# Grouped-query attention: probabilities times values in plain float32 on two column tiles, once per query tile

## The chip, the cores and the metric

The kernel runs on one core of a Trainium2 chip. The metric is the device time of one execution in microseconds (us), smaller is better. The time before is the median of three runs, 1531.39 us (1531.35 to 1532.13).

## The reference

One encoder block works on `x` of 1024 positions and 1024 channels, in float32. `x` is normalised and projected by one wide matrix; three attention branches follow (a dilated window, grouped-query attention, cross-attention to a memory of 256 rows), each is multiplied with a gate and projected, the three are merged by sigmoid gates, and a last projection closes the block. The change touches the grouped-query attention alone: eight query heads of 64 channels share two key and value heads, without a mask, over all 1024 keys.

```python
qb_ = axial_rope(rms_norm(bq.reshape(b, s, B_HEADS, HEAD_DIM), q_norm[layer]), row_pos, col_pos)
kb_ = axial_rope(rms_norm(bk.reshape(b, s, B_KV_HEADS, HEAD_DIM), k_norm[layer]), row_pos, col_pos)
vb_ = bv.reshape(b, s, B_KV_HEADS, HEAD_DIM)

def attend(qc, kb_=kb_, vb_=vb_):
    sc = jnp.einsum('bqkgd,bskd->bkgqs', qc, kb_).astype(jnp.float32) * (HEAD_DIM ** -0.5)
    p = jax.nn.softmax(sc, axis=-1).astype(vb_.dtype)
    return jnp.einsum('bkgqs,bskd->bqkgd', p, vb_)
```

## The kernel before

**Precision by splitting.** Most products run in a reduced float32 (`R`, float32r) of which two parts are kept: `split` (L104 to L106) writes a rounded part with ScalarE (ACT, L105) and the rest with VectorE (DVE, L106). A product of two split operands is three matmuls, high by high, high by low, low by high (`dense`, L143, L145, L147; `passes`, L125). The projection of the input, `dense`, has 24 matmuls of 512 columns for one half of a unit of 128 output channels, and 48 for the unit.

**The stages.** First the keys and values of the grouped-query attention (`kv_proj`, L370, with their finishing in `k_norm` and `kn_mult`), the memory's keys and values and the memory attention. Then the grouped-query attention (`b_att`, from L678 on, about 228 to 572 us of the profile). Then the dilated attention (`a_att`, `pv` at L987), the merging of the branches, and the output projection.

**Order.** TensorE's order (PE) is the program's own: a generator issues instructions and yields a cost in ns. `weave` runs two generators side by side, a queue of projection units (`dense`) and an attention; it always continues the one that is behind in its share of the whole cost. So an attention step that yields a large cost is followed by as much projection. The other engines' order is set by the tile framework's scheduler; the attention's instructions have a higher priority. Only the first part, up to the end of `kv_gen`, has ACT, DVE and POOL in program order as well.

**The values.** `kn_mult` writes the values of key tile T as `VS[:, T]`, for each of the two value heads 128 columns: the rounded part of the 64 channels (ACT, L407) and its rest (DVE, L408).

**The attention.** Keys stand on the partitions. One visit `i` is a query tile T of 128 positions and one key head, thus four query heads: 512 columns. A visit goes over eight key tiles of 128 keys in eight ticks `n`, and 128 ticks make the stage. Of different visits, one tick does these things:

- `row_max` (L688, L689): one matmul of scores with the queries on the partitions, and a minimum over 512 keys on DVE. After eight, L691 joins them.
- `shift`, nine ticks after a visit's first maximum: a transpose of the extremes (L696) and a DVE instruction (L697) that puts them beside the queries' low parts, `QL`.
- `scores`, ten ticks after: two matmuls (L706, and L707, which reads `QL`) into one PSUM bank, and the exponential on ACT (L709) to `bp`. ACT and DVE split `bp` into `bph` and `bpl`, and POOL adds the `bp` of the eight key tiles (L716, L718).
- `pv`, twelve ticks after: two matmuls into one bank of 128 rows, `VS` (rounded parts and rests side by side) by `bph` (L727) and by `bpl` (L728). Rows 0 to 63 of the bank gather the product with the rounded values, rows 64 to 127 that with the rests. After the eighth key tile ACT copies the lower half out (L731), DVE adds the upper (L732), and the sums of POOL are split.
- `final`, thirteen ticks after and at the end of a visit: the sum over the partitions of the denominators, and the DMAs of both results.

At every second visit `q_prep` transposes the next query tile (L655) and prepares `QH` and `QL` (L658 to L662). The ticks yield 216 for `row_max`, 432 for `scores`, 432 for `pv`; the projections in between are nine gate units and seven merge-gate units, whose halves are evacuated from PSUM at L212 and L213, or L220 to L222. Of the eight PSUM banks the projections have two; the attention has one bank for scores, three for maxima and transposes, and two for outputs. `BP` tiles hold exponentials, four at a time.

**Plain float32 in the same kernel.** The dilated attention's `pv` multiplies float32 values (64 columns of weights) with float32 probabilities of 128 columns, even and odd heads into rows 0 to 63 and 64 to 127 of a bank; the profile shows these as 128*64 (L987).

Of the kernel before, what the change touches and what calls it, by code (L numbers as in the profile page):

```python
# [8 lines left out]
F32 = mybir.dt.float32  # L9
R = mybir.dt.float32r  # L10
AF = mybir.ActivationFunctionType
OP = mybir.AluOpType
# [4 lines left out]
NT = 8  # L17
P = 128
# [32 lines left out]
def block(ctx: ExitStack, tc: tile.TileContext, x, xT, memT, cst, msk, bcst, tabA, gpost,  # L51
          wu, wb, wmem, wbr, wout, out):
    nc = tc.nc
    V, A, G, PE = nc.vector, nc.scalar, nc.gpsimd, nc.tensor
# [12 lines left out]
    def phase_psum(name, s2=0, s1=0, t=0, o=0):  # L67
        assert 2 * s2 + s1 + t + o <= 6
        bank["n"] = (s2, s1, t, o)
        bank["pool"] = tc.tile_pool(name=name, bufs=1, space=bass.MemoryType.PSUM, reuse_waits="tile")  # L70
        bank["p"] = bank["pool"].__enter__()

    def end_psum():
        bank["pool"].__exit__(None, None, None)
# [4 lines left out]
    def pss1():  # L79
        return bank["p"].tile([P, 512], F32, name="s1", tag="s1", bufs=bank["n"][1])  # L80

    def pst():
        return bank["p"].tile([P, 4, 128], F32, name="tr", tag="t", bufs=bank["n"][2])

    def pso():
        return bank["p"].tile([P, 512], F32, name="ov", tag="o", bufs=bank["n"][3])
# [17 lines left out]
    def split(dst_h, dst_l, src):  # L104
        A.activation(dst_h, src, AF.Copy)  # L105
        V.tensor_tensor(dst_l, src, dst_h.bitcast(F32), op=OP.subtract)  # L106
# [127 lines left out]
    def pool(name, side="left"):  # L234
        p = tc.tile_pool(name=name, bufs=1, side=side, reuse_waits="tile")
        return p, p.__enter__()
# [5 lines left out]
    kvp, kvl = pool("kvl", "right")  # L242
    mlp, ml = pool("ml", "right")
    mbp, mb = pool("mb", "right")
    KS = kvl.tile([P, 2, S], R, name="KS")
    VS = kvl.tile([P, NT, 2, 128], R, name="VS")
    kmh = ml.tile([P, 4, 256], R, name="kmh")
    kml = ml.tile([P, 4, 256], R, name="kml")
    vmh = ml.tile([P, 2, 4, 128], R, name="vmh")
# [77 lines left out]
    kt = []  # L327
# [70 lines left out]
    def kn_mult(n):  # L398
        t1, ss = part[n]
        kn = st.tile([P, 2, 2, 64], F32, name="kn", bufs=4)  # L400
        kns.append(kn)
        V.tensor_tensor(kn, t1, ss[:, :, :, None].to_broadcast([P, 2, 2, 64]), op=OP.mult)
        for t in range(2):
            T = 2 * n + t
            vv = banks[n].rearrange("q (t h d) -> q t h d", t=2, h=4)[:, t, 2:4]
            r = rcol[:, T:T + 1]
            A.activation(VS[:, T, :, 0:64], vv, AF.Copy, scale=r)  # L407
            V.scalar_tensor_tensor(VS[:, T, :, 64:128], vv, r, VS[:, T, :, 0:64].bitcast(F32),  # L408
                                   op0=OP.mult, op1=OP.subtract)

    def kv_gen(banks):
        def src(n):
# [32 lines left out]
    for k in range(8):  # L445
        if k % 2 == 0:
            load_wkv(k // 2)
        for e in range(2 if k == 0 else 1):
            t = slice(e * 512, e * 512 + 512) if k == 0 else slice(0, S)
# [29 lines left out]
    for c in range(2):  # L479
        t = st.tile([P, 4, 256], F32, name=f"mt{c}", tag=f"xk{c}")  # L480
# [6 lines left out]
    for n in range(4):  # L487
        kn_mult(n)
# [150 lines left out]
    close(mbp)  # L639
    close(mlp)  # L640
    end_psum()
    phase_psum("ps_b", s1=1, t=3, o=2)


    with tc.tile_pool(name="ba", bufs=1, reuse_waits="tile") as ba:
# [20 lines left out]
        lh = ba.tile([P, 512], R, name="blh")  # L666
        ll = ba.tile([P, 512], R, name="bll")
        lsum = [ba.tile([P, 512], F32, name=f"bl{i}") for i in range(2)]
# [9 lines left out]
        def b_att():  # L678
            st = {}

            def row_max(i, x):
                T, kv = divmod(i, 2)
                j, c = divmod(x, 2)
                if x == 0:
                    st[i] = dict(n=ba.tile([P, 4, 2], F32, name="bn2", bufs=2))
                QH, _ = QQ[T]
                s = pst().rearrange("p a b -> p (a b)")
                PE.matmul(s, QH[:, kv * 4 + j], KS[:, kv, c * 512:c * 512 + 512], start=True, stop=True)  # L688
                V.tensor_reduce(st[i]["n"][:, j, c:c + 1], s, axis=AX.X, op=OP.min)  # L689
                if x == 7:  # L690
                    V.tensor_tensor(nmt[i % 2][:, 64:68], st[i]["n"][:, :, 0], st[i]["n"][:, :, 1], op=OP.min)  # L691

            def shift(i):
                T, kv = divmod(i, 2)
                tp = pst()
                PE.transpose(tp[0:68, 0, :], nmt[i % 2], ident)  # L696
                V.tensor_tensor(QQ[T][1][64:68, 4 * kv:4 * kv + 4], tp[64:68, 0:1, :].to_broadcast([4, 4, 128]),  # L697
                                ident[64:68, 64:68, None].to_broadcast([4, 4, 128]), op=OP.mult)

            def scores(i, kt):  # L700
                T, kv = divmod(i, 2)
                d = st[i]
                QH, QL = QQ[T]
                s = pss1()
                t, h = slice(kt * 128, kt * 128 + 128), slice(4 * kv, 4 * kv + 4)
                PE.matmul(s, KS[:, kv, t], QH[:, h], start=True, stop=False)  # L706
                PE.matmul(s, KB[0:68, kv, t], QL[0:68, h], start=False, stop=True)  # L707
                pp = ba.tile([P, 512], F32, name="bp", bufs=BP)
                A.activation(pp, s, AF.Exp, scale=-1.0)  # L709
                ph = ba.tile([P, 512], R, name="bph", bufs=3)  # L710
                pl = ba.tile([P, 512], R, name="bpl", bufs=3)
                split(ph, pl, pp)
                if kt == 0:
                    d["p0"] = pp
                elif kt == 1:
                    G.tensor_tensor(lsum[i % 2], d["p0"], pp, op=OP.add)  # L716
                else:
                    G.tensor_tensor(lsum[i % 2], lsum[i % 2], pp, op=OP.add)  # L718
                d[kt] = (ph, pl)

            def pv(i, kt):
                T, kv = divmod(i, 2)
                d = st[i]
                if kt == 0:
                    d["o"] = pso()
                ph, pl = d[kt]
                PE.matmul(d["o"], VS[:, kt, kv], ph, start=kt == 0, stop=False)  # L727
                PE.matmul(d["o"], VS[:, kt, kv], pl, start=False, stop=kt == NT - 1)  # L728
                if kt == NT - 1:
                    d["ob"] = ba.tile([64, 512], F32, name="obt", bufs=2)  # L730
                    A.activation(d["ob"], d["o"][64:128], AF.Copy)  # L731
                    V.tensor_tensor(d["ob"], d["ob"], d["o"][0:64], op=OP.add)  # L732
                    split(lh, ll, lsum[i % 2])

            def final(i):
                T, kv = divmod(i, 2)
                d = st.pop(i)
                lt = pst().rearrange("p a b -> p (a b)")[0:1]
                passes(lt, [(one, x) for x in (lh, ll)])
                lr = ba.tile([1, 512], F32, name="blr", bufs=2)  # L740
                A.activation(lr, lt, AF.Copy)
                nc.sync.dma_start(lbd[4 * kv:4 * kv + 4, T * 128:T * 128 + 128], lr.rearrange("p (j q) -> p j q", j=4))
                ob = d["ob"]
                for j in range(4):
                    h = kv * 4 + j
                    nc.sync.dma_start(od[1, h // 2, (h % 2) * 64:(h % 2) * 64 + 64, T * 128:T * 128 + 128],
                                      ob[:, j * 128:j * 128 + 128])

            b_const()
            q_prep(0)  # L750
            yield 436
            for _ in range(6):
                yield 300
            for n in range(128 + LAG_F + 8):
                if n < 128:
                    i, x = divmod(n, 8)
                    row_max(i, x)
                    yield 216
                    if i % 2 and i < 15 and x == 1:
                        q_prep((i + 1) // 2)  # L760
                        yield 436
                else:
                    yield END_PAD
                if n % 8 == LAG_S % 8 and 0 <= n - LAG_S < 128:
                    shift((n - LAG_S) // 8)
                    yield 109
                m = n - LAG_T
                if m < 0:
                    yield START_PAD
                elif m < 128:  # L770
                    scores(*divmod(m, 8))
                    yield 432
                m = n - LAG_P
                if 0 <= m < 128:
                    pv(*divmod(m, 8))
                    yield 432
                m = n - LAG_F
                if m >= 0 and m % 8 == 7 and m < 128:
                    final(m // 8)
                    yield 432  # L780
# [333 lines left out]
    with tc.tile_pool(name="mg", bufs=1, reuse_waits="tile") as mg:  # L1114
# [78 lines left out]
        for m in range(len(steps) + 2):  # L1193
            if m < len(steps):
                n, i, f = steps[m]
                ths[m] = mg_unit(i, f)
            if m >= 2:
                n, i, f = steps[m - 2]
# [25 lines left out]
        for T in range(NT):  # L1224
            t = slice(T * 128, T * 128 + 128)
# [50 lines left out]
KV_K = 5  # L1276
WR, KV_STEP, RB_WAIT, KN_PAD = 2, 700, 1500, 2800.0
LAG_S, LAG_T, LAG_P, LAG_F = 9, 10, 12, 13
BP = 4
B_LEAD, B_PRIO = 1.0, 120  # L1280
G_AT = 4
ATT_PRIO = 120
# [116 lines left out]
```

## Time and profile before

| | |
|---|---|
| median of the runs | 1531.39 us |
| the profiled execution | 1529.17 us |
| its span, first to last instruction | 1527.2 us |
| mean granted TensorE clock | 0.997 |
| DVE busy | 966.0 us |
| ACT busy | 713.5 us |
| POOL busy | 429.8 us |
| DMA, mean | 78 GB/s |

The profile is one execution. A row of a group names the line, the engine, the operation, what it writes and reads, the shape and the count, then the busy time in us and the mean in ns, then the idle time of the engine ahead of it and what ended that. PEld is the weight load of a matmul, which can run while the matmul before is still going. A matmul's recorded end is modelled, so consecutive records overlap, and the pace is read from the starts. A float32r matmul is printed as f32 as well. The rows of the timeline give the start and the length of a run of equal instructions, in us.

### The profile page before, as it was taken

How to read it: one execution, taken by the hardware profiler on the slowest of the kernel's cores; microseconds unless marked ns; L12 is line 12 of the kernel's file. 1: busy time of each engine (PE TensorE's matmuls, PEld its weight loads, DVE VectorE, ACT ScalarE, POOL GpSimd, SP SyncE). 2: the span in 40 equal slices, each digit the busy share in tenths (PEclk: the TensorE clock that was granted, in tenths of full speed). 3: DMA queues.
4: the chain of work that ended last, by engine and by line, in shares of the span. 5: the costliest groups of instructions: out<-in, count | busy, mean ns of one | idle time of the engine just before them, and what ended most of it. 6: DMA issues, size and time to landing. Idle time of an engine off the chain costs nothing.

```text
span 1527.2 us, 20804 instructions
## 1 busy us (share of the span) xinstructions
PE 1493.5 (98%) x7748; PEld 1233.9 (81%) x7748; DVE 966.0 (63%) x1602; ACT 713.5 (47%) x1459; POOL 429.8 (28%) x357
## 2 busy tenths in 40 slices
PE   7899989999999999999999999999999999999998
PEld 7799977777777778888878888887888788888787
DVE  7665569999988975555566566556635442524843
ACT  6544345666677661554445445444642111212321
POOL 1425413444444552211221222122200100223422
PEclk9999999999999999999999999999999999999999
DMA  6232011111111112101121121112126541623432
GB/s 233 90 111 70 29 51 57 53 56 49 63 34 60 63 63 87 42 29 43 54 61 43 42 83 45 42 31 83 42 77 195 172 126 35 206 70 117 124 111 97
DMA packets 55044, 119.79 MB, mean 78 GB/s; under 512 B 13792, under 2 KB 23712, under 8 KB 54816
## 3 DMA queue, kind: packets, MB, share of 16 engines
q1 hardware_dynamic: 54800, 118.34, 24.4%
q8 instruction: 61, 1.00, 0.3%
q14 instruction: 39, 0.32, 0.1%
q10 hardware_dynamic: 144, 0.13, 0.0%
HBM read 96.06 MB, written 22.38 MB: 78 GB/s over the span
## 4 chain that ended last, share of the span: by engine, by line
PE 77%; DVE 10%; issue 4%; ACT 4%; POOL 3%; DMA 3%; SPq 0%; DVEq 0%; POOLq 0%; ACTq 0%
PE d L147 12%; PE d L143 12%; PE d L145 12%; PE sc L125 7%; PE sc L1246 4%; PE s L125 3%; PE sc L147 3%; PE sc L143 3%; PE sc L145 3%; PE ov L987 2%; DVE bpl L106 2%; PE ov L728 2%; PE s L707 1%; PE s L706 1%; PE ov L727 1%
## 5 line engine op out<-in xcount | busy, mean ns | idle before, releaser
L143 PE MATMUL d<-hh,wh 128*128 128x512 f32 x992 | 396.4, 400 | 5.2 <-DVE fth L222 5.2
L147 PE MATMUL d<-hh,wl 128*128 128x512 f32 x992 | 397.3, 400 | 0.0
L145 PE MATMUL d<-hl,wh 128*128 128x512 f32 x992 | 393.8, 397 | 0.0
L143 PEld LDWEIGHTS d<-hh,wh 128*128 128x128 f32 x992 | 187.3, 189 | 42.5 <-DVE fth L222 6.5
L147 PEld LDWEIGHTS d<-hh,wl 128*128 128x128 f32 x992 | 187.3, 189 | 39.0 <-issue 4.0
L145 PEld LDWEIGHTS d<-hl,wh 128*128 128x128 f32 x992 | 187.4, 189 | 36.2 <-issue 1.0
L105 ACT ACTIVATE wh<-wr 128x1024 fp32r<-128x1024 f32 (+1 forms) x100 | 95.3, 954 | 245.4 <-PE sc L145 106.0
L718 POOL TENSOR_TENSOR bl<-bl,bp 128x512 f32<-128x512 f32 x96 | 135.8, 1414 | 121.3 <-ACT bp L709 111.2
L836 POOL TENSOR_TENSOR rot<-rot,t2a 128x512 f32<-128x512 f32 x48 | 82.5, 1720 | 297.6 <-DVE t2a L835 297.6
L106 DVE TENSOR_TENSOR bpl<-bp,bph 128x512 fp32r<-128x512 f32 x128 | 131.9, 1031 | 23.6 <-ACT bph L105 23.1
L106 DVE TENSOR_TENSOR wl<-wr,wh 128x1024 fp32r<-128x1024 f32 (+1 forms) x100 | 119.0, 1190 | 21.5 <-ACT wh L105 20.8
L709 ACT ACTIVATE bp<-s 128x512 f32<-128x512 f32 x128 | 76.2, 595 | 59.9 <-PE s L707 57.8
L1147 POOL TENSOR_TENSOR acc<-acc,th 128x1024 f32<-128x1024 f32 x16 | 45.4, 2837 | 201.5 <-DVE th L1146 201.5
L945 ACT ACTIVATE pra<-pra,sts 128x128 f32<-128x128 f32 (+2 forms) x152 | 67.1, 442 | 62.3 <-DVE sts L937 61.6
L689 DVE TENSOR_REDUCE bn<-tr 128x1 f32<-128x512 f32 x128 | 86.5, 680 | 3.8 <-PE tr L688 3.3
L147 PE MATMUL sc<-hh,wl 128*128 128x512 f32 x224 | 87.3, 390 | 1.2 <-DVE wl L106 1.2
L937 DVE CUSTOM_DVE_ANT_0 pra<-s,mask 128x128 f32<-128x128 f32 (+2 forms) x152 | 48.4, 348 | 62.2 <-PE s L125 49.2
L143 PE MATMUL sc<-hh,wh 128*128 128x512 f32 x224 | 87.3, 390 | 0.0
L145 PE MATMUL sc<-hl,wh 128*128 128x512 f32 x224 | 87.1, 389 | 0.0
L105 ACT ACTIVATE bph<-bp 128x512 fp32r<-128x512 f32 x128 | 80.8, 631 | 3.5
L833 DVE TENSOR_TENSOR rot<-d,tab 128x512 f32<-128x512 f32 x48 | 33.1, 689 | 67.4 <-PE d L147 67.1
L125 PE MATMUL sc<-gh,wh 128*128 128x512 f32 x192 | 74.7, 389 | 0.0
(276 smaller groups left out, 3066.0 us busy)
## 6 DMA issues: line engine op xcount, KB each, us to landing
wr<-in_wu SPq DMA_DIRECT2D x76, 512.0 KB
g2d<-fth SPq DMA_DIRECT2D x24, 256.0 KB
wgt<-wgd SPq DMA_DIRECT2D x24, 256.0 KB
ot<-od SPq DMA_DIRECT2D x12, 512.0 KB
gt<-g2d SPq DMA_DIRECT2D x12, 512.0 KB
wr<-in_wbr SPq DMA_DIRECT2D x24, 256.0 KB
thd<-fth SPq DMA_DIRECT2D x20, 256.0 KB
th<-thd SPq DMA_DIRECT2D x10, 512.0 KB
```

The costliest lines, as they stand in the source:

```text
L105: A.activation(dst_h, src, AF.Copy)
L106: V.tensor_tensor(dst_l, src, dst_h.bitcast(F32), op=OP.subtract)
L125: PE.matmul(out_ps, a, b, start=i == 0, stop=i == n - 1)
L143: PE.matmul(dst, wh[:, k, :], hh[k][:, t], start=k == 0, stop=False)
L145: PE.matmul(dst, wh[:, k, :], hl[k][:, t], start=False, stop=False)
L147: PE.matmul(dst, wl[:, k, :], hh[k][:, t], start=False, stop=k == 7)
L689: V.tensor_reduce(st[i]["n"][:, j, c:c + 1], s, axis=AX.X, op=OP.min)
L709: A.activation(pp, s, AF.Exp, scale=-1.0)
L718: G.tensor_tensor(lsum[i % 2], lsum[i % 2], pp, op=OP.add)
L836: G.tensor_tensor(o[:, t], o[:, t], t2, op=OP.add)
L945: A.activation(src, raw, AF.Exp, scale=-1.0, bias=bias, accum_out=sts[:, h, 1, T:T + 1])
L1246: PE.matmul(parts[h], *terms[h][j], start=j == 0, stop=j == 23)
```

## The change

The values are kept as one plain float32 tile of 64 columns per head, without a rest. The probabilities aren't split; the float32 exponentials themselves are the moving operand. `pv` handles all eight key tiles of a visit in one step, in the eighth of the ticks in which it ran before: eight plain float32 matmuls of 512 columns, even key tiles into rows 0 to 63 of the bank, odd ones into rows 64 to 127. The two halves are added as before. The step yields the cost of eight former steps at once. One of the two output banks becomes a second bank for scores, and twelve exponentials are held in place of four. Everything else stays.

```diff
-    VS = kvl.tile([P, NT, 2, 128], R, name="VS")
+    VS = kvl.tile([P, NT, 2, 64], F32, name="VS")
...
-            A.activation(VS[:, T, :, 0:64], vv, AF.Copy, scale=r)
-            V.scalar_tensor_tensor(VS[:, T, :, 64:128], vv, r, VS[:, T, :, 0:64].bitcast(F32),
-                                   op0=OP.mult, op1=OP.subtract)
+            A.activation(VS[:, T], vv, AF.Copy, scale=r)
...
-    phase_psum("ps_b", s1=1, t=3, o=2)
+    phase_psum("ps_b", s1=2, t=3, o=1)
...
                 pp = ba.tile([P, 512], F32, name="bp", bufs=BP)
                 A.activation(pp, s, AF.Exp, scale=-1.0)
-                ph = ba.tile([P, 512], R, name="bph", bufs=3)
-                pl = ba.tile([P, 512], R, name="bpl", bufs=3)
-                split(ph, pl, pp)
-                if kt == 0:
-                    d["p0"] = pp
-                elif kt == 1:
-                    G.tensor_tensor(lsum[i % 2], d["p0"], pp, op=OP.add)
-                else:
+                if kt == 1:
+                    G.tensor_tensor(lsum[i % 2], d[0], pp, op=OP.add)
+                elif kt > 1:
                     G.tensor_tensor(lsum[i % 2], lsum[i % 2], pp, op=OP.add)
-                d[kt] = (ph, pl)
-
-            def pv(i, kt):
+                d[kt] = pp
+
+            def pv(i):
                 T, kv = divmod(i, 2)
                 d = st[i]
-                if kt == 0:
-                    d["o"] = pso()
-                ph, pl = d[kt]
-                PE.matmul(d["o"], VS[:, kt, kv], ph, start=kt == 0, stop=False)
-                PE.matmul(d["o"], VS[:, kt, kv], pl, start=False, stop=kt == NT - 1)
-                if kt == NT - 1:
-                    d["ob"] = ba.tile([64, 512], F32, name="obt", bufs=2)
-                    A.activation(d["ob"], d["o"][64:128], AF.Copy)
-                    V.tensor_tensor(d["ob"], d["ob"], d["o"][0:64], op=OP.add)
-                    split(lh, ll, lsum[i % 2])
+                o = pso()
+                for kt in range(NT):
+                    e = kt % 2
+                    PE.matmul(o[e * 64:e * 64 + 64], VS[:, kt, kv], d.pop(kt), start=kt < 2, stop=kt >= NT - 2)
+                d["ob"] = ba.tile([64, 512], F32, name="obt", bufs=2)
+                A.activation(d["ob"], o[64:128], AF.Copy)
+                V.tensor_tensor(d["ob"], d["ob"], o[0:64], op=OP.add)
+                split(lh, ll, lsum[i % 2])
...
                 m = n - LAG_P
-                if 0 <= m < 128:
-                    pv(*divmod(m, 8))
-                    yield 432
+                if 0 <= m < 128 and m % 8 == 7:
+                    pv(m // 8)
+                    yield 8 * 432
...
-BP = 4
+BP = 12
```

## The prediction

> **What bounds the kernel now.** I read the page's shares first, then the busy time of the engines in the stretch of the grouped-query attention, then its groups of instructions, its waits, and last single stretches of the timeline.
>
> ```profile
> span 1527.2 us, 20804 instructions
> ...
> PE 1493.5 (98%) x7748; PEld 1233.9 (81%) x7748; DVE 966.0 (63%) x1602; ACT 713.5 (47%) x1459; POOL 429.8 (28%) x357
> ```
>
> TensorE is busy nearly all the span. The attention that is changed runs from 228 to 572 us, woven with gate and filler projections. The table of stretches says for it:
>
> ```profile
> core 0: us, PE busy (x) PEld busy (x) DVE busy (x) ACT busy (x) POOL busy (x), PEclk, DMA share, GB/s
> 228.00:572.00 344.00, 337.87 (x1461) 264.23 (x1460) 313.19 (x403) 231.22 (x379) 159.60 (x113) 1.00 0.17 55
> ```
>
> PE is the bound (337.87 of 344 us), at full granted clock, but DVE is nearly as full (313.19 us, 91%). So most of the time that PE loses here should be lost to DVE. The groups of that stretch and its waits (us in total, times, longest) show what DVE does and who waits for it:
>
> ```profile
> L718 POOL TENSOR_TENSOR bl<-bl,bp 128x512 f32<-128x512 f32 x96 | 135.8, 1414 | 121.3 <-ACT bp L709 111.2 <-DVE QL L697 6.3 <-DVE bn L689 3.5
> L106 DVE TENSOR_TENSOR bpl<-bp,bph 128x512 fp32r<-128x512 f32 x128 | 131.9, 1031 | 23.6 <-ACT bph L105 23.1
> ...
> L689 DVE TENSOR_REDUCE bn<-tr 128x1 f32<-128x512 f32 x128 | 86.5, 680 | 3.8 <-PE tr L688 3.3
> L105 ACT ACTIVATE bph<-bp 128x512 fp32r<-128x512 f32 x128 | 80.8, 631 | 3.5
> ...
> L106 DVE TENSOR_TENSOR wl<-wr,wh 128x1024 fp32r<-128x1024 f32 x15 | 22.3, 1486 | 0.2 <-ACT wh L105 0.2
> ...
> L691 DVE TENSOR_TENSOR bnm<-bn 128x4 f32<-128x4 f32 x16 | 13.6, 849 | 0.4
> ...
> L697 DVE TENSOR_TENSOR QL<-tr,cs 4x512 fp32r<-4x512 f32 x16 | 11.0, 689 | 0.5
> ...
> L696 PE MATMUL tr<-cs,bnm 128*68 128x128 f32 x16 | 4.4, 275 | 1.2 <-DVE bn L689 1.2
> ```
>
> ```profile
> PEld s L706 <- ACT bp L709: 3.5, 14, 0.4
> ...
> PEld s L707 <- DVE QL L697: 3.2, 4, 1.2
> PEld ov L728 <- DVE bpl L106: 2.8, 3, 1.1
> ...
> PEld tr L696 <- DVE bn L689: 2.1, 2, 1.1
> PE s L707 <- DVE QL L697: 2.0, 4, 0.8
> ...
> PEld d L143 <- DVE fth L222: 1.7, 1, 1.7
> ...
> PE ov L728 <- DVE bpl L106: 1.5, 3, 0.7
> ...
> PE d L143 <- DVE fth L222: 1.3, 1, 1.3
> PE tr L696 <- DVE bn L689: 1.2, 2, 0.7
> ```
>
> The splitting of the probabilities is the largest DVE group (131.9 us) and costs ACT 80.8 us. Yet PE's own idle time is 2.0 + 1.5 + 1.3 + 1.2 = 6.0 us by the PE rows, and by the weight-load rows (which also count an idle loader while the last matmul still runs) 3.5 + 3.2 + 2.8 + 2.1 + 1.7 = 13.3 us. I take the middle, 9.6 us, as what the stage loses. That is the whole prize here: 213 us of removed DVE and ACT work can return at most some 10 us, because PE was the bound beside it.
>
> **Term 1, the products themselves.** Removed are 256 matmuls (L727, L728), two in each of 128 ticks. Between two ordinary matmuls they stand like this:
>
> ```profile
> 402.90 0.39 PE L145 MATMUL d<-hl,wh 128*128 128x512 f32 x1
> 403.13 0.39 PE L727 MATMUL ov<-bph,VS 128*128 128x512 f32 x1
> 403.36 0.40 PE L728 MATMUL ov<-bpl,VS 128*128 128x512 f32 x1
> 403.60 0.40 PE L147 MATMUL d<-hh,wl 128*128 128x512 f32 x1
> ```
>
> Starts are 0.233 us apart, so sixteen for one visit's worth (eight key tiles) cost 3.73 us. Added are eight plain float32 matmuls with 512 columns on alternating column tiles. The nearest rows are L987, which already does this with 128 columns. One group has sixteen products, another eight:
>
> ```profile
> 637.28 0.40 PE L143 MATMUL d<-hh,wh 128*128 128x512 f32 x1
> 637.61 1.97 PE L987 MATMUL ov<-app,avs 128*64 128x128 f32 x32
> 639.50 0.50 PE L145 MATMUL d<-hl,wh 128*128 128x512 f32 x1
> 639.84 0.39 PE L147 MATMUL d<-hh,wl 128*128 128x512 f32 x1
> ```
>
> ```profile
> 727.89 0.40 PE L145 MATMUL d<-hl,wh 128*128 128x512 f32 x1
> 728.21 1.09 PE L987 MATMUL ov<-app,avs 128*64 128x128 f32 x16
> 729.24 0.50 PE L147 MATMUL d<-hh,wl 128*128 128x512 f32 x1
> 729.58 0.40 PE L143 MATMUL d<-hh,wh 128*128 128x512 f32 x1
> ```
>
> A float32 product is two records (32 for 16). From the ordinary start ahead of a group to the second one behind it are 2.56 and 1.69 us; the 16 records between them cost 0.87 us, 0.109 for a pair of records. What is left, 2.56 - 16 x 0.109 = 0.82, less two ordinary intervals (0.46), is 0.36 us for going into the column tiles and out again. With four times the columns a pair should take 4 x 0.109 = 0.436 us if all of it is streaming, 0.429 if 2 ns of it are fixed; I take 0.43. A visit is 8 x 0.43 + 0.36 = 3.80 us against 3.73: +0.07, over 16 visits **+1.1 us**. So on PE the change saves nothing.
>
> That the 0.109 is streaming is a choice. The rows beside it in the list of forms:
>
> ```profile
> L300 PE MATMUL s<-wbh,hh 128*128 128x256 f32 x64 | 17.8, 279 | 0.0
> ...
> L987 PE MATMUL ov<-app,avs 128*64 128x128 f32 x640 | 41.5, 278 | 0.9 <-ACT app L975 0.8
> ```
>
> A float32 record of 128 columns lasts as long as an ordinary one of 256, so I read it as two array passes per column. Then the load of 64 weights hides behind it. If instead half of the 0.109 is the load, a pair of 512 columns takes 4 x 0.0545 + 0.0545 = 0.27 us and the visit 2.5. If the load is added to full streaming, a pair is 0.48 us and the visit 4.2. If the two tiles don't run side by side at 512 columns, 16 records of 0.43 make 7.2. By a page of the Trainium skill ("FP8 and Floating Point Precision", TensorE Precision Notes) true FP32 takes four passes through the array. Over two records that is two passes each, as I read the rows.
>
> **Term 2, the waits.** L728's wait for the subtract disappears with it: midpoint of its two rows, 2.15 us. The waits for L222 and for L689 (midpoints 1.5 and 1.65) are queueing behind a full DVE; it falls from 313.19 to 181 us (53%), and I take two thirds of them, 2.1 us. The load of L706 waited for ACT to empty the only score bank (3.5 us, no PE idle beside it, midpoint 1.75); with two banks I take 1.5. The wait of L707 (midpoint 2.6) I leave standing, for the reason of the first rival. Sum **-5.75 us**; bounds 0 and -13.3.
>
> New waits that I cost at nothing: the visit stands two ticks behind the last scores of its query tile, so their exponentials are done; were they late, the projections behind the visit would wait too. The one output bank is read by ACT and DVE right after the visit and needed again a whole visit (some 21 us) later. Twelve probability tiles hold the eight of a visit, two of the next and two spare. POOL's sums (7 x 1.41 = 10 us of 21) keep their order. No DMA is added or dropped; those of `final` follow at the same place of the order.
>
> **Term 3, the values.** Eight subtracts (L408) leave DVE early on. There PE waits for a gate's evacuation, which stands in DVE's order behind two of them:
>
> ```profile
> 52.48 0.34 DVE L408 SCALAR_TENSOR_TENSOR VS<-s,rcol,VS 128x128 fp32r<-128x128 f32 x1
> ...
> 53.07 0.34 DVE L408 SCALAR_TENSOR_TENSOR VS<-ov,rcol,VS 128x128 fp32r<-128x128 f32 x1
> ...
> 55.41 0.68 DVE L222 SCALAR_TENSOR_TENSOR fth<-d,fth 128x512 f32<-128x512 f32 x1
> ...
> 56.14 0.74 PE L143 MATMUL d<-hh,wh 128*128 128x512 f32 x1 [3.21 <-DVE fth L222]
> ```
>
> If that order stays, PE restarts 0.68 us sooner; a little more can come from the subtracts before. I take **-0.8 us**, bounds 0 and -3.2 (the whole wait).
>
> Sum: +1.1 - 5.75 - 0.8 = -5.4 us. The profiled execution took 1529.17 us, 2.0 over its span; that gives 1523.8. The median of the runs shown, 1531.39, is 2.2 above it, so the same difference gives **1526.0**.
>
> **The rivals.**
>
> Short ticks (slower). A tick is 344 / 128 = 2.7 us now. With the products taken out it is one row maximum, two score matmuls and about three of projection, 6 x 0.233 = 1.4 us; the time returns in a lump of 3.8 us plus as much projection once in eight ticks. But the shift is still ordered one tick ahead of the scores that need it: from L696 to L707 PE has a transpose, two scores, about four projections, a row maximum and L706, some 0.11 + 8 x 0.233 = 2.0 us. The chain between is 0.275 + up to 0.68 (a maximum in progress) + 0.689 = 1.64 us, and just before it L689 and L691 (0.68 + 0.85) must fit in two ticks. Any further DVE instruction ahead (0.68 to 1.49 us) exceeds the slack of 0.36. For it: L707 already waits at long ticks. Against it: DVE is at half load. At 0.34 us per visit (5.4 us) the gain is gone; at 0.5 to 1 us the time is 1526 + 8 to 16 = 1534 to 1542.
>
> Loads in the open, half-rate streaming not needed (faster): pair 0.27, visit 2.5, 16 x 1.3 = 21 us less than forecast: 1505. The row of 0.109 fits this as well; the length of the records speaks against it. A rule of the Trainium skill ("TensorE: Matmul & The Clock Gate", Part 3, The mechanism), that weight loads overlap running matmuls only where the row groups differ, would make this one true, since both column tiles use all rows. No row of this case settles it.
>
> Loads added to full streaming: 16 x 0.4 = 6.4 us more: 1532. Against it: 0.109 has no room for it at 128 columns.
>
> The column tiles don't run side by side: 16 x 3.4 = 55 us more: 1581. Against it: 16 records cost 0.87 us, half of what two passes per column would need one after the other (16 x 0.233 / 2 = 1.9).
>
> Nothing moves: the DVE waits shift elsewhere and cover the loss of term 1: 1531.
>
> **How the numbers follow.** Forecast 0.50, between 1521 and 1530 (of it 0.07 within the bound of no change); short ticks 0.23 (0.07 about the same, 0.16 slower); open loads 0.08; added loads 0.06 (half the same, half slower); no overlap 0.05; nothing moves 0.08. A measurement of this kernel tells 0.2%, about 3 us, from no change. So faster 0.43 + 0.08 = 0.51, the same 0.07 + 0.07 + 0.03 + 0.08 = 0.25, slower 0.16 + 0.03 + 0.05 = 0.24. The range 1518 to 1538 takes in forecast, added loads, nothing, and most of the short ticks; it leaves out open loads, no overlap and the tail of the short ticks, some 0.17.
>
> **What would show it.** Groups of 16 records on the new product line, 3.4 to 3.5 us from first to last start, and 0.36 us around them: term 1. No wait for a split, DVE near 181 us in the stage, few waits of L143 and L696: term 2. Waits at L707 or L696 above 5 us in sum: the short ticks. Groups of about 2.2 us: open loads; of 6.9: no overlap. PE restarting after a gap of under 2.6 us near 55 us: term 3. The forecast is wrong if a visit differs from 3.8 us by over 0.3, or if the stage's waits don't fall.

## The result, and the profile after

The changed kernel takes 1521.55 us (median of six runs, 1518.86 to 1524.63) against 1531.77 us of the kernel before (six runs beside them, 1531.35 to 1534.73): a ratio of 0.993, 95% interval 0.9915 to 0.9944. That is 10.2 us less; forecast were 5.4. The profiled execution took 1522.17 us, 7.0 less than the profiled one before. The first fence is the page of the changed kernel, the second its row in the table of stretches (columns as in the prediction).

```profile
span 1520.3 us, 20465 instructions
...
PE 1492.1 (98%) x7748; PEld 1203.8 (79%) x7748; DVE 840.7 (55%) x1466; ACT 633.9 (42%) x1331; POOL 421.4 (28%) x357
```

```profile
228.00:572.00 344.00, 342.74 (x1495) 239.72 (x1494) 189.73 (x272) 152.88 (x252) 152.07 (x115) 1.00 0.18 58
```

DVE fell from 313.19 to 189.73 us in the stretch, ACT from 231.22 to 152.88, and PE is now busy for 342.74 of 344. To place the time I cut the span at two instructions of the program that both kernels have: the first row maximum (`tr<-KS,QH`) and the first transpose of the dilated attention's values (`tr<-cs,vta`). The view of one tile gives first and last start of each; before, then after:

```profile
L688 PE MATMUL tr<-KS,QH x128: 388/394/472, 228.2 to 543.0; 128*128 128x512 f32 x128
...
L911 PE MATMUL tr<-cs,vta x76: 270/271/273, 611.1 to 1114.1; 128*128 128x128 f32 x76
```

```profile
L686 PE MATMUL tr<-KS,QH x128: 388/395/468, 224.6 to 529.4; 128*128 128x512 f32 x128
...
L902 PE MATMUL tr<-cs,vta x76: 270/271/273, 600.4 to 1103.4; 128*128 128x128 f32 x76
```

The start is 228.2 - 224.6 = 3.6 us shorter. The stage between the marks, with the attention and its projections, went from 382.9 to 375.8 us: 7.1 less. The dilated attention kept its length (536.5 us between its first value transpose and the first matmul of the merging, in both). In the merging (from its first matmul to the first of the output projection) this execution lost 3.4 us that nearly all the others did not: the rest of a weight (`wl`, DVE, L106) came late once, TensorE stood idle for 2.75 us and, a little later, ran at half its pace for a while.

```profile
1178.63 0.50 PE L147 MATMUL sc<-hh,wl 128*128 128x512 f32 x1 [2.75 <-DVE wl L106]
...
1180.34 0.63 PE L147 MATMUL sc<-hh,wl 128*128 128x512 f32 x1
1180.76 0.63 PE L143 MATMUL sc<-hh,wh 128*128 128x512 f32 x1
```

The starts are 0.43 us apart in place of 0.23. The merging took 287.9 us here, 284.5 before, and 284.3 to 285.6 in eleven of the twelve profiles of the experiments; the twelfth had the same gap (2.76 us). So 3.6 + 7.1 is what the change itself gives in the trace, near the 10.2 us of the medians.

**The products.** A visit in the timeline of the changed kernel:

```profile
248.24 0.40 PE L143 MATMUL d<-hh,wh 128*128 128x512 f32 x1
248.56 3.65 PE L720 MATMUL ov<-bp,VS 128*64 128x512 f32 x16
252.15 0.50 PE L145 MATMUL d<-hl,wh 128*128 128x512 f32 x1
252.48 0.39 PE L147 MATMUL d<-hh,wl 128*128 128x512 f32 x1
```

From 248.24 to 252.48 are 4.24 us; less two ordinary intervals, 3.78 us for a visit, forecast 3.80. The two records of a pair start 0.007 us apart, the pairs 0.429. So a record of 512 columns takes nearly twice the 0.231 us of an ordinary one, which fits two passes per column but doesn't prove them; two records run side by side; and the weight loads (0.137 us each) add nothing that shows, since the pair of 128 columns took 0.109 and four times that is 0.436.

**The waits** of the same stretch, all that the matmuls' own rows (PE) show:

```profile
PE s L704 <- ACT bp L707: 0.7, 1, 0.7
PE s L705 <- DVE QL L695: 0.6, 2, 0.3
```

PE's idle time fell from 6.0 to 1.3 us. A second measure goes by the starts of the matmuls: of every interval longer than 0.262 us, what it has over 0.231 counts as lost (intervals at column tiles and transposes left out). By it the stage lost 10.2 us before and 2.4 after: 7.8 less. With 16 x (3.78 - 3.73) = +0.8 for the products that is the 7.1 of the stage.

**The start.** In the changed kernel the gate's evacuation (L222) stands behind one subtract of the weights (L507) and no longer behind rests of the values:

```profile
51.04 1.22 DVE L507 TENSOR_TENSOR wl<-wr,wh 128x1024 fp32r<-128x1024 f32 x1
52.17 0.68 DVE L222 SCALAR_TENSOR_TENSOR fth<-d,fth 128x512 f32<-128x512 f32 x1
...
52.91 0.50 PE L143 MATMUL d<-hh,wh 128*128 128x512 f32 x1 [1.73 <-DVE fth L222]
```

The idle time went from 3.21 to 1.73 us. And behind the gap of before stood a cost that the prediction did not count: in these rows of before, then after, the granted clock is the third number from the end.

```profile
56.10:59.60 3.50, 3.46 (x8) 2.75 (x9) 3.01 (x8) 1.54 (x2) 0.77 (x1) 0.52 0.80 219
```

```profile
53.00:56.00 3.00, 3.00 (x14) 2.46 (x15) 2.95 (x5) 1.01 (x2) 1.20 (x2) 1.00 0.88 240
```

After 3.21 us of idle time the clock was 0.52 over 3.5 us; after 1.73 us it stayed at 1.00. Behind this the changed kernel is 4.8 us ahead (the same matmul of L147 starts at 54.86 and 59.66 us). Of that 1.2 us are lost again before the first row maximum, the larger part near 211 us, where its clock is 0.50 for 6.8 us, against 3.4 us before.

### The profile page after: what moved, and what is told of

Read it like the earlier page. It is cut to its first block, busy times and chain, and to the rows that moved or that the text cites. A ratio compares the mean times of both kernels' runs of the same rounds, so it can differ in the third digit from the quotient of the medians.

```text
span 1520.3 us, 20465 instructions
## 1 busy us (share of the span) xinstructions
PE 1492.1 (98%) x7748; PEld 1203.8 (79%) x7748; DVE 840.7 (55%) x1466; ACT 633.9 (42%) x1331; POOL 421.4 (28%) x357
## 4 chain that ended last, share of the span: by engine, by line
PE 83%; DVE 5%; issue 3%; DMA 3%; ACT 3%; POOL 3%; SPq 0%; POOLq 0%; DVEq 0%; ACTq 0%
PE d L147 13%; PE d L145 13%; PE d L143 13%; PE sc L125 7%; PE ov L720 4%; PE sc L1237 4%; PE s L125 3%; PE sc L147 3%; PE sc L145 3%; PE sc L143 3%; PE s L705 2%; PE ov L978 2%; PE s L704 2%; PE tr L686 2%; DMA wgt<-wgd 2%
## 5 line engine op out<-in xcount | busy, mean ns | idle before, releaser
L143 PE MATMUL d<-hh,wh 128*128 128x512 f32 x992 | 396.5, 400 | 1.7 <-DVE fth L222 1.7
L147 PE MATMUL d<-hh,wl 128*128 128x512 f32 x992 | 397.2, 400 | 0.0
L147 PEld LDWEIGHTS d<-hh,wl 128*128 128x128 f32 x992 | 187.0, 188 | 41.9 <-issue 7.6
L143 PEld LDWEIGHTS d<-hh,wh 128*128 128x128 f32 x992 | 187.0, 189 | 41.0 <-issue 3.2
L711 POOL TENSOR_TENSOR bl<-bl,bp 128x512 f32<-128x512 f32 x96 | 128.6, 1339 | 142.1 <-ACT bp L707 137.4
L106 DVE TENSOR_TENSOR wl<-wr,wh 128x1024 fp32r<-128x1024 f32 (+1 forms) x100 | 116.9, 1170 | 22.2 <-ACT wh L105 21.4
L707 ACT ACTIVATE bp<-s 128x512 f32<-128x512 f32 x128 | 75.2, 594 | 84.8 <-PE s L705 84.5
L147 PE MATMUL sc<-hh,wl 128*128 128x512 f32 x224 | 88.0, 393 | 2.8 <-DVE wl L106 2.8
L143 PE MATMUL sc<-hh,wh 128*128 128x512 f32 x224 | 87.8, 392 | 0.0
L125 PE MATMUL sc<-gh,wl 128*128 128x512 f32 x192 | 74.8, 390 | 0.0
L125 PE MATMUL sc<-gl,wh 128*128 128x512 f32 x192 | 74.7, 389 | 0.0
```

The lines of the kernel that those rows point to most:

```text
L125: PE.matmul(out_ps, a, b, start=i == 0, stop=i == n - 1)
L143: PE.matmul(dst, wh[:, k, :], hh[k][:, t], start=k == 0, stop=False)
L147: PE.matmul(dst, wl[:, k, :], hh[k][:, t], start=False, stop=k == 7)
```

## The experiments

Of each run the stage and its start are given as above, in us, and the ratio to the kernel before on the same chip with its 95% interval. The times are medians.

| run | time | before, same chip | ratio | start | stage |
|---|---|---|---|---|---|
| changed | 1521.55 | 1531.77 | 0.993 (0.9915 to 0.9944) | 224.6 | 375.8 |
| split back | 1558.63 | 1529.73 | 1.0184 (1.0168 to 1.0199) | 224.8 | 416.1 |
| DVE's half | 1553.26 | 1529.73 | 1.0146 (1.0131 to 1.0161) | 225.2 | 409.3 |
| ACT's half | 1522.59 | 1529.73 | 0.995 (0.9931 to 0.9969) | 225.3 | 376.5 |
| rests of the values back | 1524.46 | 1529.73 | 0.9963 (0.995 to 0.9976) | 229.5 | 375.8 |
| pairs | 1536.57 | 1531.65 | 1.0035 (1.0025 to 1.0046) | 225.1 | 392.1 |
| pairs, split back | 1539.38 | 1531.65 | 1.005 (1.0034 to 1.0067) | 225.8 | 393.5 |
| not alternating | 1548.23 | 1531.65 | 1.0105 (1.0085 to 1.0125) | 225.0 | 404.0 |
| one score bank | 1547.56 | 1531.65 | 1.0099 (1.0084 to 1.0114) | 224.4 | 401.1 |
| before, two score banks | 1559.73 | 1530.06 | 1.019 (1.0174 to 1.0206) | 227.2 | 414.9 |
| two visits at once | 1520.46 | 1530.06 | 0.9937 (0.9924 to 0.995) | 225.7 | 376.5 |
| even ticks | 1519.51 | 1530.06 | 0.9931 (0.9918 to 0.9945) | 224.3 | 374.8 |
| pairs, split back, one score bank | 1544.88 | 1530.65 | 1.0099 (1.0081 to 1.0117) | 225.0 | 400.1 |

The theory at first was the prediction's: TensorE waited for a full DVE, and the change emptied it. The rival was that the waits went with the products' dependence on the splits, or with the banks.

**The split put back.** In `scores`, behind the exponential:

```diff
+                ph = ba.tile([P, 512], R, name="bph", bufs=3)
+                pl = ba.tile([P, 512], R, name="bpl", bufs=3)
+                split(ph, pl, pp)
```

> The changed kernel, with the split of the probabilities put back (128 rounded copies on ACT, 128 subtracts on DVE into two tiles that nothing reads); the products stay plain float32 in one visit. Theory (the stage lost time because TensorE waited for a full DVE, and that load is what the change took away): the stage from the first row maximum to the first value transpose of the dilated attention goes from 375.8 us back towards 383, by 5 to 9 us, and the whole to 1527 to 1531. Rival (the waits went because the products no longer read the splits, and because scores have a second bank; DVE's load as such is harmless): the stage stays within 1.5 us of 375.8 and the whole near 1522.

Measured: the stage took 416.1 us, 40 more. Neither had expected that. Its row and its waits:

```profile
228.00:572.00 344.00, 317.97 (x1326) 214.36 (x1325) 289.22 (x376) 210.23 (x350) 148.82 (x104) 0.98 0.15 48
```

```profile
PE s L705 <- DVE QL L695: 13.1, 11, 2.3
PEld tr L694 <- DVE bnm L689: 10.9, 9, 2.9
PE tr L694 <- DVE bnm L689: 7.0, 9, 2.5
```

These are the two links of the prediction's first rival: the extremes joined on DVE (L689) for the shift (L694), and DVE's result (L695) for the second score matmul (L705). DVE is less busy in these 344 us than before the change (289 against 313 us), and yet TensorE waits much more.

**Half of it each.** Only DVE's subtract, or only ACT's copy:

```diff
+                pl = ba.tile([P, 512], R, name="bpl", bufs=3)
+                V.tensor_tensor(pl, pp, pp, op=OP.subtract)
```

```diff
+                ph = ba.tile([P, 512], R, name="bph", bufs=3)
+                A.activation(ph, pp, AF.Copy)
```

> The changed kernel with only DVE's half of the old load: 128 subtracts of 128x512 from the exponentials into a tile that nothing reads. Theory (DVE is the engine that TensorE waited for): nearly all of what putting back both halves costs, 5 to 9 us on the stage. Rival (ACT's queue, which empties the score banks, was the cause): within 1.5 us of the changed kernel.

> The changed kernel with only ACT's half of the old load: 128 copies of 128x512 into a tile that nothing reads. Theory (DVE is the cause): the stage stays within 1.5 us of 375.8. Rival (ACT is the cause): 3 us or more on the stage.

DVE's half cost 33.5 us on the stage, ACT's 0.7. So nearly all of it is DVE's half, as the theory said, at several times its price.

**The visit cut into pairs**, without and with the split. In `pv(i, kp)` only two key tiles are multiplied, and the order has

```diff
-                if 0 <= m < 128 and m % 8 == 7:
-                    pv(m // 8)
-                    yield 8 * 432
+                if 0 <= m < 128 and m % 2 == 1:
+                    pv(m // 8, m % 8 // 2)
+                    yield 2 * 432
```

> The changed kernel with the visit cut into four: two float32 products (one on each column tile) in every second tick, each paying its own way into the column tiles and out. Theory (0.36 us for each stay in the column tiles, a pair of records at 0.43 us): 64 stays in place of 16, so 48 x 0.36 = 17 us more on the stage, 375.8 to 393, and the whole near 1538. Rival (the 0.36 us is an end effect that overlaps with other work, and even ticks help the other engines): within 5 us of the changed kernel.

> As the run in pairs, and the split of the probabilities put back on ACT and DVE into tiles that nothing reads. The split cost 40 us on the stage when the products came in one visit (375.8 to 416.1). Theory (the split's load hurts through the short ticks: 0.69 + 1.03 us of DVE in a tick of 1.4 us of TensorE; with the products spread, the tick is long enough): the split costs here 5 to 12 us over the run in pairs, about the waits that the kernel before had. Rival (the load hurts in any order): 30 us or more over the run in pairs.

The pairs cost 16.3 us on the stage, near the 17 expected. One of them in the timeline, 1.68 us from the first line's start to the last's, less two intervals 1.22 = 2 x 0.43 + 0.36:

```profile
245.21 0.40 PE L145 MATMUL d<-hl,wh 128*128 128x512 f32 x1
245.54 1.08 PE L722 MATMUL ov<-bp,VS 128*64 128x512 f32 x4
246.55 0.50 PE L147 MATMUL d<-hh,wl 128*128 128x512 f32 x1
246.89 0.40 PE L143 MATMUL d<-hh,wh 128*128 128x512 f32 x1
```

The split on top cost 1.4 us, against 40 with whole visits and 5 to 12 expected. Its row, and the largest waits that aren't a change of the column tiles:

```profile
228.00:572.00 344.00, 342.98 (x1418) 218.69 (x1417) 307.80 (x393) 224.02 (x370) 154.26 (x110) 1.00 0.16 54
```

```profile
PEld tr L125 <- DVE bll L106: 2.2, 3, 0.8
...
PE tr L125 <- DVE bll L106: 0.5, 2, 0.3
```

DVE is busy 307.80 us, as full as before the change, and TensorE hardly waits. So the load as such is harmless; what matters is where in the order it falls. With whole visits, the ticks between them last 1.4 us of TensorE by the prediction's count, and a tick's row minimum and subtract need 0.68 + 0.98 us of DVE (their means in that run). In pairs the time of the products stands between the ticks. This also speaks against my first theory for the gain: DVE's load by itself doesn't make the 7.8 us of waits.

**Not alternating.** The order of the key tiles in a visit:

```diff
-                for kt in range(NT):
+                for kt in (0, 2, 4, 6, 1, 3, 5, 7):
```

> The changed kernel with the eight products of a visit ordered 0, 2, 4, 6, 1, 3, 5, 7, so that four products in a row go to the same column tile. Theory (the two column tiles run side by side only when neighbours in the order go to different ones, and a record of 512 columns takes 0.43 us alone): 15 of the 16 records follow one another, a visit takes 6.9 us in place of 3.44 and the stage 16 x 3.2 to 3.4 = 51 to 55 us more, the whole near 1575. Rival (records of one tile overlap as well): no change.

```profile
248.64 0.40 PE L143 MATMUL d<-hh,wh 128*128 128x512 f32 x1
248.97 5.42 PE L720 MATMUL ov<-bp,VS 128*64 128x512 f32 x16
254.32 0.50 PE L145 MATMUL d<-hl,wh 128*128 128x512 f32 x1
254.65 0.39 PE L147 MATMUL d<-hh,wl 128*128 128x512 f32 x1
```

A visit takes 6.01 - 0.46 = 5.55 us, 1.77 more, and 16 of them are the 28.2 us of the stage. Both were wrong. The single starts show why: 248.97, 249.45, 249.88, 250.30, then 250.73 and 250.74 together, three more such pairs, and four alone again. So the first four records run alone, about 0.43 us apart, then eight run in four pairs. The records of both column tiles bear one name, so which is which is a reading: when the fifth of the first tile starts, the first of the other tile, ninth in the order, starts beside it.

**One score bank** in the changed kernel, `phase_psum("ps_b", s1=1, t=3, o=2)`:

> The changed kernel with the old division of the banks: one bank for scores, two for outputs. Theory (with ticks of 1.4 us the scores of a tick must wait until ACT has emptied the only bank, 0.6 us of exponential and its latencies; the second bank took that away): 3 to 10 us more on the stage. Rival (the bank is free again a tick later in any case, and DVE alone counted): within 1.5 us of 375.8.

```profile
PEld s L704 <- ACT bp L707: 36.7, 73, 2.5
...
PE s L704 <- ACT bp L707: 16.2, 19, 2.1
```

The stage is 25.3 us longer, where 3 to 10 were expected. With ticks as short as this the second bank isn't an extra; without it the change would have been slower than before (ratio 1.0099).

**The kernel before with two score banks**, `phase_psum("ps_b", s1=2, t=3, o=1)`:

> The kernel before with one edit: two banks for scores and one for outputs, as in the changed kernel; probabilities split, two products per tick. The split put back in pairs cost 1.4 us, with DVE 308 us busy of 344, so DVE's load alone doesn't explain the 8 us of waits that the change removed. Theory (the single score bank did: scores waited for ACT, and everything behind them came later): the stage falls from 382.9 by 5 to 8 us, the waits for DVE of L696, L707 and L143 go with it, and the whole is near 1524. Rival (the products' own dependence on the split did, and nothing but plain float32 removes it): the stage falls by less than 3 us and L728 still waits.

```profile
PE ov L727 <- DVE obt L732: 24.4, 14, 3.4
...
PE s L707 <- DVE QL L697: 1.6, 4, 0.5
PE tr L696 <- DVE bn L689: 1.2, 2, 0.6
```

The stage grew by 32 us, which neither side had expected, for a reason that I had overlooked: with a product in every tick the next visit writes the only output bank one tick after the last, and must wait for DVE's L732. In the changed kernel it is needed a whole visit later, and no such wait appears. The waits of L707 and L696 stood nearly unchanged, so a second score bank alone doesn't take them away; but with so much else waiting, this run can't settle it.

**The pairs with the split and one score bank** settle more: load and score bank as before, and products that don't read the splits. Two more things differ from the kernel before: three times the exponentials are held, and the 64 pairs take 64 x 1.22 = 78 us where the 256 products of before took 60, so that a tick has 0.14 us more of TensorE's time.

> The run in pairs with the split put back (stage 393.5 us, hardly a wait), with one bank for scores and two for outputs as in the kernel before. Now load, order and banks are nearly those of before, and only the products don't read the splits. Theory (the 8 us of waits before came from products that read the splits: TensorE stood at L728, and what followed came late): the stage stays within 2 us of 393.5. Rival (the single score bank caused them): the stage is 4 to 9 us longer, with waits for ACT at the scores and for DVE behind them.

```profile
PEld s L704 <- ACT bp L707: 12.6, 35, 1.5
PE s L704 <- ACT bp L707: 2.3, 6, 1.0
...
PE s L705 <- DVE QL L695: 0.3, 1, 0.3
```

The stage is 6.6 us longer than with two banks, as the rival said, but nearly all of that is waiting for ACT. DVE's waits of before (L696 1.2, L143 1.3, L728 1.5, L707 2.0 us in PE's rows) don't come back. So a single score bank doesn't bring them. That of L728 (`bpl`) went by construction, since the new products read no split. The others went with the products' reading of the splits, with the twelve exponentials in place of four, or with the longer ticks of this run; no run separates these.

**The rests of the values**, made again into a tile of their own that nothing reads, by the eight DVE instructions of before:

```diff
+            V.scalar_tensor_tensor(VL[:, T], vv, r, VS[:, T], op0=OP.mult, op1=OP.subtract)
```

> The changed kernel with the eight DVE instructions put back that made the rests of the values, into a tile of their own that nothing reads. Theory (they stood in DVE's and ACT's order ahead of the gate evacuation that TensorE waited for near 50 us, and the gap of over 3 us that this made also cost half-clock time): the first row maximum, now at 224.6 us, comes 2 to 4 us later, the gap of TensorE near 53 us is over 3 us again, and the stage itself stays at 375.8. Rival (the start merely fell differently in this execution): the first row maximum stays within 1 us of 224.6.

```profile
52.83 2.15 DVE L509 TENSOR_TENSOR wl<-wr,wh 128x1024 fp32r<-128x1024 f32 x1
54.91 0.68 DVE L222 SCALAR_TENSOR_TENSOR fth<-d,fth 128x512 f32<-128x512 f32 x1
...
55.64 0.80 PE L143 MATMUL d<-hh,wh 128*128 128x512 f32 x1 [3.21 <-DVE fth L222]
```

The stage starts 4.9 us later, where 2 to 4 were expected; the gap is 3.21 us again to the hundredth, and from 55.7 to 61.7 us the granted clock was 0.50. The weights' subtract (L509) takes 2.15 us here as before, 1.22 in the changed kernel (L507). So the eight instructions are what the start gained by: in the eleven traces without them the stage begins at 224.3 to 225.8 us, in the three with them at 227.2 to 229.5.

**Two variants of the change.** Two visits in one stay of sixteen products, with two banks each for scores, maxima and outputs and twenty exponentials; and the visit's cost yielded evenly:

```diff
-                if 0 <= m < 128 and m % 8 == 7:
-                    pv(m // 8)
-                    yield 8 * 432
+                if 0 <= m < 128:
+                    if m % 8 == 7:
+                        pv(m // 8)
+                    yield 432
```

> The changed kernel with two visits (both key heads of a query tile) in one stay of sixteen products, two banks each for scores, for maxima and for outputs, twenty exponentials held. Theory (0.36 us for each stay): eight stays fewer, 2.9 us less on the stage, if two banks are enough for the maxima: the stage at 373 and the whole at 1518 to 1519. Rival (with ticks of 1.4 us the maxima need the third bank, as the scores need the second): DVE's minimum holds TensorE up at the row maxima and the stage is 5 us or more longer.

> The changed kernel with the cost of the visit yielded over its eight ticks (432 each), so that projections are spread evenly over the ticks in place of a lump behind the visit: a tick outside the visit is 1.9 us in place of 1.4. Theory (the rest of the waits, about 2 us, comes from the short ticks): the stage 1 to 2 us shorter, the whole about 1520 to 1521. Rival (what waits are left have another cause): within 0.5 us of 375.8 on the stage.

Two visits at once took 7.68 - 0.46 = 7.22 us in place of 2 x 3.78, as the 0.36 of a stay says, so 2.7 us were saved. Yet the stage is 0.7 longer, less than the rival's 5, since maxima and shifts now wait:

```profile
PEld tr L686 <- DVE QL L695: 1.8, 4, 0.7
PEld tr L686 <- DVE bn L687: 1.7, 4, 0.6
PEld tr L694 <- DVE bn L687: 1.6, 3, 1.0
```

Even ticks took 1.0 us off the stage, the lower end of what was expected. Both ratios overlap that of the changed kernel; neither is shown to be faster than it.

## Why the prediction was right, point by point

**The sign and the range** held: 1521.55 lies between 1518 and 1538, and within the forecast's own 1521 to 1530, at its lower end. The gain was 10.2 us, forecast 5.4. Only term 1 was right in both mechanism and size. That the time still lies in the range is in part luck: it had room for nearly twice the forecast gain.

**Term 1 (+1.1)** measured +0.8, by a visit of 3.78 us. The scaling of the pair from 128 to 512 columns held (0.429, where 0.43 was taken), and the 0.36 us for a stay held for 2, 8 and 16 products. The rivals with weight loads in the open (2.5 us), with loads added (4.2) and without overlap (7.2) are refuted. The rule of the Trainium skill ("TensorE: Matmul & The Clock Gate", Part 3, The mechanism) that a weight load overlaps a running matmul only with other row groups doesn't hold here as it stands: both column tiles use all rows, and 16 records of 512 columns show no time for their loads.

**Term 2 (-5.75)** measured -7.8. The step that failed is "The wait of L707 (midpoint 2.6) I leave standing": by the matmuls' starts it fell from 3.6 to 1.0 us. Its reason, the slack of 0.36 us on short ticks, was sound as a danger: with the split put back the waits stand at just these links, and the stage is 40 us longer. But with DVE relieved it didn't arise. By the same measure L728 gave 2.0 us (forecast 2.15), L143 and L696 together 3.4 (forecast 2.1), and L706 nothing: it lost 0.3 us before and 0.8 after, where 1.5 were to be gained. And the cause I named for the waits of L143 and L696, DVE's load, doesn't make them by itself: the same load in pairs costs 1.4 us. What made them, the products' reading of the splits, the number of exponentials or the length of the ticks, stays open.

**A small item hid a large one.** For the second score bank I took 1.5 us, from the waits of long ticks. On the short ticks that the change makes, leaving it out costs 25.3, more than the whole gain.

**Term 3 (-0.8)** is the term of the sum that was most mis-sized: the start gained 3.6 us, more than the bound of 3.2, and putting the rests back costs 4.9. I counted two instructions of 0.34 us. TensorE went on 3.2 us sooner in the two profiles. Of that 0.7 us were there at 41 us, ahead of the first rest, and in this execution of before alone. The other 2.5 us every trace has: from DVE's instruction L402 near 41 us to the evacuation (L222) are 13.65 us with the rests and 11.15 without, within 0.02. They are 1.05 us that ACT's copies and DVE's rests, alternating on the same banks, had put DVE's chain back by; 0.5 of the two rests; and 0.9 because the weights' subtract took 1.2 in place of 2.15 us. Left out too was that the gap of 3.2 us was paid twice, by the gap and by the clock after it (0.52 over 3.5 us, 1.7 us lost).

**"Nothing moves"** fell with terms 2 and 3.

## What to carry to other kernels

On a kernel that TensorE bounds, price the new matmuls first, from the nearest row that the trace has, way in and out included: here as many records, each nearly twice as long but two side by side, cost the same, and only then did the freed engines count. When work is gathered into one place, look at the order that it was gathered out of: a bank or an engine that had room in the old, longer steps may have none in the short ones left behind (here 25 us for one bank, and 33.5 us for one DVE subtract per tick). The parts of such a change can hold one another up, so price them together: the output bank was free for a second score bank only because the products were gathered, and the gathered form needed that bank.

## What the runs showed of the hardware that was not expected

- With four products in a row for one column tile and then four for the other, 16 records took the time of 12, about 0.43 us each: four alone, four pairs, four alone. Read by the order, the other tile's first record started beside the fifth of the first tile, though eight stood before it: TensorE ran ahead across column tiles, here by a distance of four records.
- After 3.21 us of idle time (and after 2.75 us in the merging) TensorE's matmuls came 0.43 us apart for some microseconds; after 1.73 us they did not. But the length of the gap alone doesn't decide it: with one score bank the granted clock was 0.50 over 3.4 us behind a gap of 2.08 us (at 315.7 us), and with DVE's half it stayed at 1.00 behind one of 2.41 us (at 540.3 us).
- The same subtract of 128x1024 on DVE (L507, or L509) took 1.22 us in some traces and 2.15 in others, beside an addition on POOL (L393). In the eleven traces where the subtract began first, by 0.3 us, it took 1.22 us and the addition 2.03; in the three where the addition began first, by 0.2 us, the subtract took 2.15 and the addition 1.27. So whichever began first was short and the other was held up; no run tried the two apart.
